# Stick-breaking attention as two lanes of 24 key blocks, and twelve projections as six pairs by seven products

## The chip, the core and the metric

The kernel runs on one core of a Trainium2 chip. Its engines are TensorE (PE, with its weight loads PEld), VectorE (DVE), ScalarE (ACT), GpSimd (POOL) and SyncE (SP), whose queue issues most of the DMAs. The metric is the device time of one execution in microseconds; lower is better. A time is given as the median of several runs.

## What is computed

One layer of a hybrid decoder trunk for 1024 tokens of width 1024, in float32. A normalised input goes through one input projection, and three mixers work on its parts: a state space model (SSD), stick-breaking attention and sparse attention (NSA). Each mixer's output is projected, scaled by a sigmoid gate, and summed; an output projection and a gated MLP follow. The edit touches the stick-breaking attention, the projections that feed it and the gates:

```python
def stick_breaking_attention(qkv):          # 4 heads of 128, blocks of 128 queries
    ...
    for i in range(s // SB_QBLK):
        q0 = i * SB_QBLK
        kl = q0 + SB_QBLK
        qb = q[:, :, q0:kl]
        zl = jnp.einsum('bhqd,bhkd->bhqk', qb, k[:, :, :kl]).astype(jnp.float32) * scale
        mask = jnp.arange(kl)[None, :] < (q0 + jnp.arange(SB_QBLK))[:, None]
        ls = jax.nn.log_sigmoid(zl)
        lk = jnp.where(mask, ls - zl, 0.0)
        later = lax.cumsum(lk, axis=3, reverse=True) - lk
        w = jnp.where(mask, jnp.exp(ls + later), 0.0)
        outs.append(jnp.einsum('bhqk,bhkd->bhqd', w.astype(v.dtype), v[:, :, :kl]))
...
        gm = jax.nn.sigmoid(merge_gate.astype(jnp.float32)).reshape(bsz, s, 3, D_MODEL)
        mixed = (gm[:, :, 0] * (y_ssm @ w_br_ssm[l]) + gm[:, :, 1] * (y_sb @ w_br_sb[l])
                 + gm[:, :, 2] * (y_nsa @ w_br_nsa[l])).astype(x.dtype)
```

## The kernel before

**Products.** Every float32 operand is split into a high and a low part, and a product is made of three matmuls (high by high, high by low, low by high). A *unit* is 128 output channels of the input projection: for each of two halves of 512 tokens, eight slices of 128 inputs times three matmuls, 48 matmuls of 128x512 into one bank `dense` (`fm_unit`; `half_unit` is the same as a generator that yields after every slice, three matmuls, so that other work can be put between: a *fine step*). `load_w` (lines 282 to 293) fetches a unit's weights on SP, copies the high part on ScalarE and subtracts on GpSimd (`whi`, `wlo`).

**Pairs.** `ssm_units` (line 586) does the 24 units of the SSD in twelve pairs: two units by two halves are a 2 by 2 block product, made with seven products of 12 matmuls each, 84 instead of 96. Its weights are combined in `weights7`, its inputs once in `combos` into the tiles `x`, 36 of them, which are given up at the end of this stage (`early.close()`).

**The stages.** The program goes through: input norm and the first projections; gate unit 0 and the SSD's twelve pairs; NSA, between whose matmuls the gate units 1 to 11 are filled in; the stick-breaking attention (`sb_stage`, line 1124); the SSD's scan; the branch projections, the output projection and the MLP. A gate tile is a `dense` bank through three ScalarE passes (`sigmoid`: exp, ln, exp, tile `gate_e`) and is stored to memory.

**The attention.** `project(h)` makes q, k and v of a head from three units, with the key columns 32 and 127 swapped, as six row tiles of 128x1024 (high and low part each; two sets of them exist). A `chain` is one head and one half c of the queries (512 columns) against key blocks of 128 from the last one down: eight blocks for c = 1, four for c = 0. A block goes through three steps: `score` (three matmuls into a bank, VectorE's minimum, ScalarE's exp and ln, its copy z, VectorE's maximum), `carry` (VectorE subtracts the row carried over from the block before, ScalarE and GpSimd split into `s_hi`, `s_lo`, two matmuls with a triangle sum up), `value` (VectorE adds the sum to z, ScalarE's exp, the split into `w_hi`, `w_lo`, three matmuls into the output bank). Blocks on the diagonal use 256 or 384 columns. A chain has two banks for scores (`ps_s` for c = 1, `ps_t` for c = 0) and one for its output (`ps_o`, `ps_b`). `attend(h)` takes one step of the chain c = 1 and, every second time, one of c = 0, and after each step some fine steps of a filler: the projection of the next head and two gates, at a rate of `SB_FILL` a step. Head 0's projection stands ahead of it without anything beside; behind each head what is left of its filler is finished before the next begins. Gates 12 to 23 are spread over the four heads, the last two behind a wait for value matmuls (`issue_after`).

A scheduler puts the recorded instructions in a static order per engine, and every engine works in that order. In NSA the order is as written.

Of the kernel before, what the change touches and what calls it, by code (L numbers as in the profile page):

```python
# [19 lines left out]
T = 1024  # L20
# [152 lines left out]
SB_GATES = (12, 14, 16, 18, 22, 24)  # L173

SB_LATE = 24
# [8 lines left out]
SB_FILL = (2.2, 2.2, 2.2, 2)  # L184
# [26 lines left out]
def trunk(ctx: ExitStack, tc: tile.TileContext, A: dict, outT: bass.AP, dbg=None):  # L211
# [362 lines left out]

    def gates(j0, j1, steps=unit_steps):
        for j in range(j0, j1):
            def evict(h, ps):
                e = gp.tile([128, 512], F32, name="gate_e")
                sigmoid(e, ps)
                nc.sync.dma_start(g_d[j * 128:(j + 1) * 128, hs(h)], e)  # L580
            yield from steps(U_GATE + j, evict)


    s_d = scratch("s_d", [24 * 128, T])

    def ssm_units():
# [26 lines left out]
        for q, m in itertools.product(range(4), (0, 2, 1)):  # L613
            u0 = 6 * q + 2 * m
            halos = [ev.tile([128, 4], F32, name="halo", bufs=4) for _ in range(2)]

            def evict(n, h, ps):
                o = ev.tile([128, 512], F32, name="o")
                if m < 2:
                    cu = q * 4 + 2 * m + n  # L620
                    conv(o, h, ps, [pvc(PV_CW, 4 * cu + 3 - d) for d in range(4)], pvc(PV_CB, cu), halos[n])
                act(o, o if m < 2 else ps, AF.Silu)
                nc.sync.dma_start(s_d[(u0 + n) * 128:(u0 + n + 1) * 128, hs(h)], o)

            w = weights7(wx, A["wfm"][U_SSM + u0], A["wfm"][U_SSM + u0 + 1], 512)
# [19 lines left out]

    ssm_units()
    tc.keep_in_program_order(nc.scalar.preload_act_table_set(TABLE))
# [476 lines left out]
def sb_stage(nc, tc, es, env):  # L1124
# [5 lines left out]

    def project(h, res):
        q_hi, q_lo, k_hi, k_lo, v_hi, v_lo = [row_t(n, R32) for n in range(6)]
        v_hi, v_lo = [x.rearrange("p (t d) -> p t d", d=128) for x in (v_hi, v_lo)]
        res.extend((q_hi, q_lo, k_hi, k_lo, v_hi, v_lo))

        def ev_q(c, ps):
            s = E.hs(c)
# [3 lines left out]
        def ev_k(c, ps):  # L1141
            s = E.hs(c)
# [7 lines left out]
        def ev_v(c, ps):  # L1150
            vT = hd.tile([128, 512], F32, name="half")
# [12 lines left out]
        for n, ev in enumerate((ev_q, ev_k, ev_v)):  # L1164
            yield from E.fine_steps(E.U_SB + 3 * h + n, ev)

    def chain(h, c, ps_z, ps_out, q_hi, q_lo, k_hi, k_lo, v_hi, v_lo):

        def tl(nm, dt=F32, bufs=None):
            return wk.tile([128, 512], dt, name=nm, tag=f"{nm}{c}", bufs=bufs)  # L1170

        po = ps_out()
        top = 4 * c + 3
        st = {}

        def cols(kb):
            j = kb - 4 * c
            return j, min(max(j, 0) * 128, 256), slice(kb * 128, (kb + 1) * 128)

        def strict(x, kb):  # L1180

            j, c0, _ = cols(kb)
# [4 lines left out]
        def score(kb):  # L1187
            _, c0, ks = cols(kb)
# [4 lines left out]
            mm(pz[:, c0:], k_lo[:, ks], q_hi[:, qs], start=False, stop=True)  # L1193
# [8 lines left out]
            strict(a, kb)  # L1202
            st[kb] = pz, a, z

        def carry(kb):
            _, c0, _ = cols(kb)
            pz, a, _ = st[kb]
            if kb < top:
                b0 = cols(kb + 1)[1]
                row = a[SWAP[0]:SWAP[0] + 1, b0:]  # L1210
                V.tensor_tensor(row, row, st[kb + 1][0][0:1, b0:], op=OP.subtract)
# [6 lines left out]
            mm(pz[:, c0:], E.neg_tri_r, s_lo[:, c0:], start=False, stop=True)  # L1218

        def value(kb):  # L1220
            _, c0, _ = cols(kb)
            pz, _, z = st[kb]
            V.tensor_tensor(z[:, c0:], z[:, c0:], pz[:, c0:], op=OP.add)
            act(z[:, c0:], z[:, c0:], AF.Exp)
            strict(z, kb)
# [4 lines left out]
            for n, (l, r) in enumerate(((v_hi, w_hi), (v_lo, w_hi), (v_hi, w_lo))):  # L1230
                last[0] = mm(po[:, c0:], l[:, kb, :], r[:, c0:], start=kb == top and n == 0, stop=kb == 0 and n == 2,
                   skip_group_check=True)
# [6 lines left out]
        y = wk.tile([128, 512], F32, name="ysb", bufs=2)  # L1239
        act(y, po, AF.Copy)  # L1240
        nc.sync.dma_start(E.y_d[(8 + h) * 128:(9 + h) * 128, c * 512:(c + 1) * 512], y)

    def attend(h, fill, late, *qkv):
        gens = [chain(h, 1, ps_s, ps_o, *qkv), chain(h, 0, ps_t, ps_b, *qkv)]
        n = m = i = 0
        while gens:
            for x in list(gens):
                if len(gens) == 2 and x is gens[1] and n % 2:
                    continue
                if next(x, 0) == 0:  # L1250
                    gens.remove(x)
                m += SB_FILL[h]
                fill.take(int(m))
                m -= int(m)
                i += 1
# [655 lines left out]
```

## Time and profile before

| | us |
|---|---|
| median of 3 runs | 2240.0 (2238.74 to 2242.33) |
| span of the profiled execution | 2244.0 |
| first to twelfth pair of the SSD, by product 3 | 108.4 to 317.2 |
| transposes of `nac` at the end of NSA | 814.1 |
| first score of the attention, `ps_t` and `ps_s` | 828.3 and 834.5 |
| last value product of the attention | 1148.3 |

The page gives the span, from the first to the last instruction, as the profiled execution's time; it stands 4.0 us above the median. PE, PEld, DVE, ACT and POOL are busy for 97, 77, 59, 54 and 57% of it. Matmuls are pipelined and overlap in the trace, and so do element passes that follow each other on one engine; the pace of an engine is then read from the distance of starts. The trace's windows give busy time with overlaps counted once, the granted TensorE clock (1.00 is full speed) and the share of the DMA engines. Rows of DMAs stand under SPq, the queue that issues them.

### The profile page before, as it was taken

Reading aid. Unit: us, or ns where it says so; the run is one execution under the profiler, and the core shown is the slowest. Engines: PE = TensorE matmul, PEld = TensorE weight load, DVE = VectorE, ACT = ScalarE, POOL = GpSimd, SP = SyncE. Lnnn points to the kernel's source line nnn. Section 1 sums busy time; section 2 is a strip of 40 time slices with the busy share of each in tenths; the row PEclk is TensorE's granted clock in tenths of the full one; section 3 lists DMA queues with packets and bytes.
Section 4 is the critical chain, followed back from the end, with each engine's and each line's share of the span. In section 5 each row is a group of like instructions: output and inputs, shape, how many; then the busy total and the mean of one; then the engine's idle time right before and its main releaser. Section 6 shows DMA issues by size and latency. Waiting matters only on the chain.

```text
span 2244.0 us, 30112 instructions
## 1 busy us (share of the span) xinstructions
PE 2167.6 (97%) x10589; PEld 1731.7 (77%) x10589; DVE 1314.7 (59%) x2419; ACT 1204.4 (54%) x2240; POOL 1269.3 (57%) x1122
## 2 busy tenths in 40 slices
PE   7999999999999999999999999999999999999997
PEld 7888889876666688888776678888778888878887
DVE  6765545257557426556537662228955767675776
ACT  6544442467757746667755531236644444575534
POOL 3777641146746734333337646568686777765743
PEclk9999999999999999999999999999999999999999
DMA  5233341321221011112262264235332323255433
GB/s 174 82 113 108 113 134 55 111 84 35 55 75 34 13 57 41 64 59 88 99 216 87 81 219 141 88 128 184 116 99 80 118 94 113 99 187 175 141 104 118
DMA packets 120104, 234.64 MB, mean 105 GB/s; under 512 B 28816, under 2 KB 43088, under 8 KB 119952
## 3 DMA queue, kind: packets, MB, share of 16 engines
q1 hardware_dynamic: 117072, 230.13, 31.2%
q10 hardware_dynamic: 2880, 2.59, 0.3%
q8 instruction: 83, 1.36, 0.3%
q14 instruction: 69, 0.57, 0.1%
HBM read 169.10 MB, written 63.57 MB: 104 GB/s over the span
## 4 chain that ended last, share of the span: by engine, by line
PE 80%; DVE 6%; ACT 4%; POOL 3%; issue 3%; DMA 2%; SPq 0%; DVEq 0%; ACTq 0%; POOLq 0%
PE dense L219 55%; PE ps_s L219 7%; PE ps_o L219 7%; PE ps_t L219 6%; PE ps_b L219 4%; PE psn L219 3%; DVE u L329 1%; POOL wlo L292 1%; POOL wlo L538 0%; DMA wraw<-in_wfm 0%; ACT dec L1302 0%; ACT wT L1000 0%; DMA traw<-in_wtm 0%; POOL h_lo L472 0%; DVE x L1530 0%
## 5 line engine op out<-in xcount | busy, mean ns | idle before, releaser
L292 POOL TENSOR_TENSOR wlo<-wraw,whi 128x256 fp32r<-128x256 f32 x344 | 273.1, 825 | 274.3 <-ACT whi L287 274.1
L219 PE MATMUL dense<-h_hi,whi 128*128 128x512 f32 x656 | 262.6, 400 | 0.0
L219 PE MATMUL dense<-h_hi,wlo 128*128 128x512 f32 x656 | 256.7, 392 | 1.2 <-POOL wlo L538 1.2
L219 PE MATMUL dense<-h_lo,whi 128*128 128x512 f32 x656 | 256.5, 391 | 0.0
L1011 POOL TENSOR_TENSOR wT_lo<-wT,wT_hi 128x512 fp32r<-128x512 f32 x132 | 168.8, 1288 | 84.8 <-ACT wT_hi L1010 76.5
L219 PE MATMUL dense<-hi,whi 128*128 128x512 f32 x576 | 214.5, 391 | 1.3 <-ACT whi L287 1.3
L219 PE MATMUL dense<-hi,wlo 128*128 128x512 f32 x512 | 200.8, 394 | 0.5 <-POOL wlo L292 0.4
L219 PE MATMUL dense<-x,uhi 128*128 128x512 f32 x600 | 191.8, 392 | 2.7 <-ACT uhi L546 1.5
L219 PE MATMUL dense<-lo,whi 128*128 128x512 f32 x448 | 176.1, 393 | 0.0
L287 ACT ACTIVATE whi<-wraw 128x1024 fp32r<-128x1024 f32 (+1 forms) x94 | 92.6, 985 | 154.4 <-PE dense L219 125.3
L547 POOL TENSOR_TENSOR ulo<-uf,uhi 128x1024 fp32r<-128x1024 f32 x38 | 91.8, 2416 | 115.0 <-ACT uhi L546 109.6
L219 PEld LDWEIGHTS dense<-h_hi,wlo 128*128 128x128 f32 x656 | 123.1, 188 | 27.9 <-POOL wlo L538 1.6
L219 PEld LDWEIGHTS dense<-h_hi,whi 128*128 128x128 f32 x656 | 123.7, 189 | 23.4
L219 PEld LDWEIGHTS dense<-h_lo,whi 128*128 128x128 f32 x656 | 123.5, 188 | 22.7
L219 PEld LDWEIGHTS dense<-x,uhi 128*128 128x128 f32 x600 | 112.4, 188 | 28.4 <-ACT x L610 2.4
L1215 POOL TENSOR_TENSOR s_lo<-sa,s_hi 128x512 fp32r<-128x512 f32 (+2 forms) x48 | 53.7, 1119 | 139.7 <-ACT s_hi L1214 139.7
L219 PEld LDWEIGHTS dense<-hi,whi 128*128 128x128 f32 x576 | 108.4, 188 | 25.5 <-ACT whi L287 2.1
L972 DVE TENSOR_REDUCE mx<-ps_t 128x1 f32<-128x384 f32 (+3 forms) x192 | 98.7, 520 | 48.9 <-PE ps_t L219 46.0
L329 DVE SCALAR_TENSOR_TENSOR u<-dense,pv,u 128x511 f32<-128x511 f32 (+1 forms) x140 | 103.5, 741 | 34.5 <-ACT u L325 34.5
L219 PEld LDWEIGHTS dense<-hi,wlo 128*128 128x128 f32 x512 | 96.3, 188 | 23.7 <-POOL wlo L292 2.0
L550 POOL TENSOR_TENSOR ulo<-uf,uhi 128x1024 fp32r<-128x1024 f32 x38 | 91.8, 2415 | 39.6 <-ACT uhi L549 38.0
L538 POOL TENSOR_TENSOR wlo<-wraw,whi 128x1024 fp32r<-128x1024 f32 x38 | 92.8, 2441 | 30.2 <-ACT whi L537 30.1
(555 smaller groups left out, 6088.4 us busy)
## 6 DMA issues: line engine op xcount, KB each, us to landing
wraw<-in_wfm SPq DMA_DIRECT2D x62, 512.0 KB, 3.7
wraw<-in_wup SPq DMA_DIRECT2D x52, 512.0 KB, 3.5
lo<-m_d SPq DMA_DIRECT2D x58, 256.0 KB, 3.2
g_d<-gate_e SPq DMA_DIRECT2D x48, 256.0 KB, 2.0
s_d<-o SPq DMA_DIRECT2D x48, 256.0 KB, 2.0
ge<-g_d SPq DMA_DIRECT2D x24, 512.0 KB, 3.4
m_d<-u SPq DMA_DIRECT2D x44, 256.0 KB, 2.0
row<-s_d SPq DMA_DIRECT2D x16, 512.0 KB, 5.0
```

Of the source, the lines that this page charges most:

```text
L219: i = f(*a, **k)
L287: act(hi, raw, AF.Copy)
L292: (V if tiles else P).tensor_tensor(lo[:, s], raw[:, s], fl(hi[:, s]), op=OP.subtract)
L329: V.scalar_tensor_tensor(o[:, d:], ps[:, :512 - d], taps[d], o[:, d:], op0=OP.mult, op1=OP.add)
L538: P.tensor_tensor(wlo, raws[0], fl(whi), op=OP.subtract)
L547: P.tensor_tensor(l24, f24, fl(h24), op=OP.subtract)
L550: P.tensor_tensor(l31, f31, fl(h31), op=OP.subtract)
L972: V.tensor_reduce(mx[:, h, a, n:n + 1], pm[:, :w], axis=AX, op=OP.max)
L1011: P.tensor_tensor(lo, wf, fl(hi), op=OP.subtract)
L1215: (P if SB_SLO else V).tensor_tensor(s_lo[:, c0:], a[:, c0:], fl(s_hi[:, c0:]), op=OP.subtract)
```

## The change

The units of gates 12 to 17 and of q, k, v of heads 0 and 1 are now made in six pairs behind the SSD's twelve, in the first stage. The gates' tiles go through `gate_out` as before. The heads' rows are stored to a scratch tensor `p_d`, and `fetch(h)` loads them in the attention stage, splits q and k, and transposes and splits v. Both fetches stand ahead of the chains.

The chains become two lanes of 24 blocks each, which go on from one head to the next: lane 0 does (head 0, c = 1), (1, 0), (2, 1), (3, 0); lane 1 does (0, 0), (1, 1), (2, 0), (3, 1). Both take all their steps in each of 26 turns. Left as filler are three gates, the units of heads 2 and 3, and three gates: twelve units, of which twelve fine steps stand ahead of the lanes. The rate of fill is 0.8 fine steps a step in turns 0 to 7, 2 in turns 8 to 15, and 0.7 behind; by turns 8, 12 and 16 at least 3, 6 and 9 units must be done. Every fill stands behind a matmul six marks back (`issue_after`).

```diff
-SB_GATES = (12, 14, 16, 18, 22, 24)
-
-SB_LATE = 24
+PAIR_GATES = 12, 18
+N_KEPT = 2
+SB_GATES = 18, 21, 24
+
+SB_DUE = {8: 3, 12: 6, 16: 9}
+SB_LEAD = 6
+SB_AHEAD = 12
...
-SB_FILL = (2.2, 2.2, 2.2, 2)
+SB_RATE = (0.8, 0.8, 2, 2, 0.7, 0.7)
...
+        tc.keep_in_program_order(nc.scalar.preload_act_table_set(TABLE))
+
+        def kept(u, h, ps):
+            o = ev.tile([128, 512], F32, name="o")
+            if u % 3 == 0:
+                act(o, ps, AF.Copy, scale=SB_SCALE)
+            else:
+                act(o, ps, AF.Copy)
+                dst, src = [x.rearrange("p (t k) -> p t k", k=128) for x in (o, ps)]
+                for m, n in (SWAP, SWAP[::-1]):
+                    act(dst[:, :, m], src[:, :, n], AF.Copy)
+            nc.sync.dma_start(p_d[u * 128:(u + 1) * 128, hs(h)], o)
+
+        for m, u in enumerate(range(0, 3 * N_KEPT, 2)):
+            pair(U_SB + u, m, lambda n, h, ps: kept(u + n, h, ps))
+        for m, j in enumerate(range(*PAIR_GATES, 2)):
+            pair(U_GATE + j, m, lambda n, h, ps: gate_out(j + n, h, ps))
...
+    def fetch(h, res):
+
+        rows = [row_t(n, R32) for n in range(6)]
+        for n in range(3):
+            r = (3 * h + n) * 128
+            nc.sync.dma_start(fl(rows[2 * n + 1]), E.p_d[r:r + 128, :])
+        for n in range(2):
+            hi, lo = rows[2 * n:2 * n + 2]
+            act(hi, fl(lo), AF.Copy)
+            V.tensor_tensor(lo, fl(lo), fl(hi), op=OP.subtract)
+            yield
+        hi, lo = rows[4:]
+        for c in range(2):
+            pt = E.psd.tile([128, 512], F32, name="dense", tag="dense")
+            for j in range(4):
+                s = slice((4 * c + j) * 128, (4 * c + j + 1) * 128)
+                tr(pt[:, j * 128:(j + 1) * 128], fl(lo[:, s]), ident)
+            act(hi[:, E.hs(c)], pt, AF.Copy)
+            V.tensor_tensor(lo[:, E.hs(c)], pt, fl(hi[:, E.hs(c)]), op=OP.subtract)
+            yield
...
-        for n in range(top + 3):
+        for n in range(len(blocks) + 2):
             for f, m in ((carry, n - 1), (value, n - 2), (score, n)):
-                if 0 <= m <= top:
-                    f(top - m)
-                    yield
...
+                if 0 <= m < len(blocks):
+                    f(m)
+                    yield True
+            yield False
...
+    marks = []
+    st = [[] for _ in range(4)]
+    for h in range(N_KEPT):
+        E.Fill(fetch(h, st[h])).rest()
+    fill = Units([gate(j) for j in range(SB_GATES[0], SB_GATES[1])] +
+                 [u for h in range(N_KEPT, 4) for u in project(h, st[h])] +
+                 [gate(j) for j in range(SB_GATES[1], SB_GATES[2])])
+    order = [[(0, 1), (1, 0), (2, 1), (3, 0)], [(0, 0), (1, 1), (2, 0), (3, 1)]]
+    lanes = [lane(l, [(h, c, kb) for h, c in hc for kb in range(4 * c + 3, -1, -1)], z, o)
+             for l, (hc, z, o) in enumerate(zip(order, (ps_s, ps_t), (ps_o, ps_b)))]
+    fill.ahead()
+    fill.take(SB_AHEAD)
+    due = 0
+    for t in range(26):
+        if t in SB_DUE:
+            fill.until(SB_DUE[t])
+        if t == 20:
+            E.ssm_rows(0, range(6))
+        on = list(lanes)
+        while on:
+            for x in list(on):
+                if not next(x):
+                    on.remove(x)
                     continue
...
+                due += SB_RATE[min(t // 4, 5)]
+                fill.ahead()
+                with tc.issue_after(marks[-SB_LEAD].ins) if len(marks) >= SB_LEAD else nullcontext():
+                    fill.take(int(due))
+                due -= int(due)
+    with tc.issue_after(marks[-1].ins):
+        fill.take(1000)
```

What this does to the order of instructions is shown at three places. The first is TensorE at the end of NSA, at the transpose of `nac` (the SSD's decay, the last matmul of that stage). Before:

```order
L219 MATMUL dense<-h_lo,whi 128x512
L219 MATMUL dense<-h_hi,wlo 128x512
L219 MATMUL dense<-h_hi,whi 128x512
L219 MATMUL ps_b<-ident,nac 128x128
L219 MATMUL dense<-h_lo,whi 128x512
L219 MATMUL dense<-h_hi,wlo 128x512
L219 MATMUL dense<-h_hi,whi 128x512
```

There `dense<-h_hi,whi` and its like are matmuls of head 0's projection. After the change:

```order
L223 MATMUL ps_b<-dta,tab 128x128
L223 MATMUL ps_b<-ident,nac 128x128
L223 MATMUL ps_s<-row_9348,row_9350 128x256
L223 MATMUL ps_s<-row_9349,row_9350 128x256
L223 MATMUL ps_t<-row_9348,row_9350 128x256
L223 MATMUL ps_t<-row_9349,row_9350 128x256
L223 MATMUL ps_s<-row_9348,row_9350 128x256
L223 MATMUL ps_s<-row_9349,row_9350 128x256
L223 MATMUL ps_t<-row_9348,row_9350 128x256
L223 MATMUL ps_t<-row_9349,row_9350 128x256
L223 MATMUL dense<-ident,row_9353 128x128 x8
L223 MATMUL ps_s<-row_9348,row_9351 128x256
```

Here `row_9348` and `row_9349` are the high and low part of head 0's q, `row_9350` and `row_9351` those of its k, `row_9353` and `row_9380` the fetched v of heads 0 and 1. The rows that follow the transpose of `nac` now all read fetched rows; the next dense matmul stands behind the sixteen transposes of v.

The second place is SP's queue there, after the change (`y_d<-yT` is NSA's last output, `ac_d` holds the decays):

```order
L1075 DMA y_d<-yT 128x2x128
L1145 DMA ac_d<-ac_9333 128x128
L1145 DMA ac_d<-ac_9334 128x128
L582 DMA g_d<-gate_e 128x512
L289 DMA wraw<-in_wfm 128x1024
L1162 DMA row_9349<-p_d 128x1024
L1162 DMA row_9351<-p_d 128x1024
L1162 DMA row_9353<-p_d 128x1024
L1162 DMA row_9376<-p_d 128x1024
L1162 DMA row_9378<-p_d 128x1024
L1162 DMA row_9380<-p_d 128x1024
```

Before, weight loads follow at this place; now the six fetches do, behind the store of the last filled gate half and the weight load of gate 20.

The third place is TensorE within the attention. Before, in head 2 with both chains under way (`row_9430` to `row_9433` are its q and k, `row_9434` and `row_9435` its v):

```order
L219 MATMUL ps_s<-row_9430,row_9432 128x512
L219 MATMUL ps_s<-row_9431,row_9432 128x512
L219 MATMUL ps_s<-row_9430,row_9433 128x512
L219 MATMUL ps_s<-s_hi,rtab 128x384
L219 MATMUL dense<-h_hi,whi 128x512
L219 MATMUL dense<-h_lo,whi 128x512
L219 MATMUL dense<-h_hi,wlo 128x512
L219 MATMUL dense<-h_hi,whi 128x512
L219 MATMUL ps_s<-s_lo,rtab 128x384
L219 MATMUL ps_o<-w_hi,row_9434 128x256
L219 MATMUL ps_o<-w_hi,row_9435 128x256
L219 MATMUL dense<-h_lo,whi 128x512
```

After, near the end, with lane 0 in head 3 (`row_10480` and `row_10481` its q, `row_10620` and `row_10621` its k, `row_10777` and `row_10778` its v):

```order
L223 MATMUL ps_s<-s_lo,rtab 128x256
L223 MATMUL ps_b<-w_lo,row_10777 128x512
L223 MATMUL ps_s<-row_10480,row_10620 128x384
L223 MATMUL ps_s<-row_10481,row_10620 128x384
L223 MATMUL ps_s<-row_10480,row_10621 128x384
L223 MATMUL ps_s<-s_hi,rtab 128x256
L223 MATMUL ps_s<-s_lo,rtab 128x256
L223 MATMUL dense<-h_hi,whi 128x512
L223 MATMUL dense<-h_lo,whi 128x512
L223 MATMUL dense<-h_hi,wlo 128x512
L223 MATMUL ps_o<-w_hi,row_10777 128x256
L223 MATMUL ps_o<-w_hi,row_10778 128x256
```

Before, dense matmuls stand between the two triangle matmuls and between the value products, and ten more follow the rows shown; after, three stand in the step. From the first score to the last value product the order has 1026 dense matmuls before and 546 after.

More of the change, by code (lines that the diff above doesn't have):

```diff
@@ L611, in snap, with pair @@
             return t
[L613 to L625, printed above, removed]
+        def pair(u, m, evict):
+            w = weights7(wx, A["wfm"][u], A["wfm"][u + 1], 512)
             x, y, z, v = ps_d(), ps_s(), ps_t(), (ps_o, ps_b)[m % 2]()
@@ L1185, in strict, with score @@
                 V.tensor_tensor(x[:, dg], x[:, dg], E.sb_mask[:, 256 - (dg.stop - c0):], op=OP.min)
-        def score(kb):
-            _, c0, ks = cols(kb)
+        def score(n):
+            h, c, _ = blocks[n]
+            _, c0, ks = cols(n)
+            q_hi, q_lo, k_hi, k_lo = st[h][:4]
             qs = slice(c * 512 + c0, (c + 1) * 512)
@@ L1239, in chain @@
[L1239 to L1248, printed above, removed]
-                    continue
[L1250 to L1255, printed above, removed]
-                if late and i > SB_LATE:
-                    with tc.issue_after(last[0].ins):
-                        late.take(2)
-            n += 1
@@ L1261, in sb_stage @@
[L1261 to L1275 removed]
+            for m, (x, y) in enumerate(((v_hi, w_hi), (v_lo, w_hi), (v_hi, w_lo))):
+                last = mm(po[0][:, c0:], x[:, kb, :], y[:, c0:], start=kb == top and m == 0, stop=kb == 0 and m == 2,
+                          skip_group_check=True)
@@ new lines, in value, with __init__, ahead, steps @@
+            marks.append(last)
+            if kb == 0:
+                y = wk.tile([128, 512], F32, name="ysb", bufs=2)
+                act(y, po[0], AF.Copy)
+                nc.sync.dma_start(E.y_d[(8 + h) * 128:(9 + h) * 128, c * 512:(c + 1) * 512], y)
+        for n in range(len(blocks) + 2):
+            for f, m in ((carry, n - 1), (value, n - 2), (score, n)):
+                if 0 <= m < len(blocks):
+                    f(m)
+                    yield True
+            yield False
+    class Units:
+        def __init__(self, units):
+            self.units, self.ready, self.cur, self.begun = list(units), [], None, 0
+        def ahead(self):
+            if self.units and not self.ready:
+                start, u, evict = self.units.pop(0)
+                self.ready.append((E.load_w(A["wfm"][u], 1024), start, evict))
+        def steps(self):
+            w, start, evict = self.ready.pop()
+            start()
+            self.begun += 1
+            for h in range(2):
+                out = []
+                yield from E.half_unit(E.psd, w, E.h_rhs, 8, h, out)
+                evict(h, out[0])
+        def step(self):
+            if self.cur is None:
+                self.ahead()
+                if not self.ready:
+                    return 0
+                self.cur = self.steps()
+            if next(self.cur, 0) != 0:
+                return 1
+            self.cur = None
+        def take(self, n):
+            while n > 0:
+                did = self.step()
+                if did == 0:
+                    return
+                n -= did or 0
+        def until(self, n):
+            while self.begun < n or self.cur:
+                self.step()
```

103 lines of the change are left out of this document (53 added, 50 removed).

## The prediction

> **What bounds the kernel now.** I read the page's totals first, then the chain of work that ended last, then windows over the two stages that the edit touches.
>
> ```profile
> span 2244.0 us, 30112 instructions
> ...
> PE 2167.6 (97%) x10589; PEld 1731.7 (77%) x10589; DVE 1314.7 (59%) x2419; ACT 1204.4 (54%) x2240; POOL 1269.3 (57%) x1122
> ...
> PE 80%; DVE 6%; ACT 4%; POOL 3%; issue 3%; DMA 2%; SPq 0%; DVEq 0%; ACTq 0%; POOLq 0%
> ```
> TensorE holds 80% of the chain, so a matmul less is worth its issue interval, as long as TensorE does not begin to wait. Matmuls overlap in the trace, so that interval is the distance of two starts:
>
> ```profile
> 803.15 0.39 PE L219 MATMUL dense<-h_hi,wlo 128*128 128x512 f32 x1
> 803.37 0.39 PE L219 MATMUL dense<-h_hi,whi 128*128 128x512 f32 x1
> 803.60 0.39 PE L219 MATMUL dense<-h_lo,whi 128*128 128x512 f32 x1
> ...
> 834.46 0.87 PE L219 MATMUL ps_s<-row,row 128*128 128x256 f32 x6
> ...
> 1148.29 0.39 PE L219 MATMUL ps_o<-w_lo,row 128*128 128x512 f32 x1
> ```
> A 128x512 matmul takes 0.2265 us of issue here. The last two rows are the first scores of the long lane and the last value product of the attention: its stage runs from 834.5 to 1148.5 us, 314.0 us. The windows show how full it is:
>
> ```profile
> core 0: us, PE busy (x) PEld busy (x) DVE busy (x) ACT busy (x) POOL busy (x), PEclk, DMA share, GB/s
> 127.74:317.18 189.44, 188.26 (x817) 152.85 (x816) 104.06 (x166) 88.82 (x130) 126.13 (x79) 1.00 0.33 109
> 828.28:1148.52 320.24, 315.08 (x1458) 259.08 (x1456) 180.73 (x331) 212.78 (x441) 116.92 (x134) 1.00 0.22 74
> 940.33:970.50 30.17, 28.88 (x138) 23.85 (x137) 25.68 (x47) 24.39 (x54) 13.29 (x14) 1.00 0.12 36
> ```
> The first is ten pairs of the seven-product stage (from the third product of one pair to that of the tenth after it): 18.94 us a pair, which is 84 matmuls at 0.2255 us, with ScalarE at 47% and GpSimd at 67%. The second is the attention: TensorE 98% busy, ScalarE only 66%, VectorE 56%. So before, the attention's element work is covered by dense projections and gates. The third is a stretch in which both chains of one head run: there VectorE is at 85% and ScalarE at 81%, and TensorE falls to 96%.
>
> **The change, part by part.**
>
> *Six pairs instead of twelve units.* Six pairs are added to the first stage: 6 x 18.94 = 113.6 us. Their extra ScalarE work (three passes for each of four gate tiles) has room beside 47%; the twelve stores of 256 KB and six loads of 512 KB have room beside a DMA share of 0.33; without that cover the passes would cost about 7 us a gate pair. Ahead of the first scores 120 of head 0's 144 dense matmuls go (the order has the last 24 behind them), and four transposes: -27.2 - 0.5 us. So the first score moves by 113.6 - 27.7 = +85.9 us, plus the wait that follows. Twelve plain units are 576 matmuls, six pairs 504: 72 x 0.2265 = 16.3 us less TensorE work in all.
>
> *The fetch.* Head 0 and 1 now come from memory, and TensorE's next row behind the transpose of nac reads them; before, dense rows stood there. The loads stand on SP behind the store of the last gate half and a weight load. The rows that price this:
>
> ```profile
> 807.43 1.06 ACT L287 ACTIVATE whi<-wraw 128x1024 fp32r<-128x1024 f32 x1
> 808.40 0.58 ACT L262 ACTIVATE gate_e<-dense 128x512 f32<-128x512 f32 x1
> ...
> 810.86 0.32 SPq L580 DMA_DIRECT2D g_d<-gate_e  x1
> 811.48 0.33 SPq L285 DMA_DIRECT2D wraw<-in_wfm  x1
> ...
> DMA to landing us min/median/max: 3.7/5.3/6.4
> ...
> L1428 DVE TENSOR_TENSOR row<-row,row 128x1024 fp32r<-128x1024 f32 x2 | 2.4, 1218 | 0.0
> ```
> Count from the last dense matmul of the gates. The weight copy ahead ends 1.0 us later, the gate's three passes and its store take 810.86 - 808.40 = 2.5 us more, the weight load follows, and the first row is issued at about 4.4 us. The landing line is that of four row loads of 512 KB in one burst (1057.5 to 1059.3 us); here the first two land after 4.9 and 5.7 us. Then ScalarE copies q and k (1.06 us each): first score at 11.7 us. TensorE has 2 us of its own until then, so it waits 9.7 us. The sixth row lands at about 15.4 us; its halves, VectorE's subtractions of 1.2 us and the two dense banks hold the next dense row to about 19.6 us, with 3.2 us of TensorE work since the first score: another 4.7 us. I take 14 us; the bounds are 8 (loads at the 3.7 us minimum, second wait hidden) and 17 (at 6.4 us). Queued behind TensorE's waiting row are all scores and all dense rows; nothing else can cover it.
>
> *The lanes.* 48 blocks stay 48, with the same passes. What goes is the half pace of the short chain and the ends between heads; what also goes is cover: between first score and last value 546 dense matmuls stand instead of 1026, twelve units fewer. I counted the order in 24 steps, from one score of lane 0 to the next, and gave each instruction its start-to-start time. Two such times, and the scores of a two-lane stretch:
>
> ```profile
> 966.12 0.65 ACT L1214 ACTIVATE s_hi<-sa 128x512 fp32r<-128x512 f32 x1
> 966.64 0.64 ACT L1224 ACTIVATE sz<-sz 128x512 f32<-128x512 f32 x1
> ...
> 950.30 0.69 DVE L1196 TENSOR_SCALAR sa<-ps_s 128x512 f32<-128x512 f32 x1 [0.52 <-PE ps_s L219]
> 950.90 0.64 DVE L1185 TENSOR_TENSOR sz<-sz,tab 128x128 f32<-128x128 f32 x1
> 951.67 0.69 DVE L1196 TENSOR_SCALAR sa<-ps_t 128x512 f32<-128x512 f32 x1
> ...
> 960.34 0.68 DVE L1196 TENSOR_SCALAR sa<-ps_s 128x512 f32<-128x512 f32 x1
> 960.94 0.41 DVE L1196 TENSOR_SCALAR sa<-ps_t 128x256 f32<-128x256 f32 x1
> ...
> 963.23 0.42 DVE L1196 TENSOR_SCALAR sa<-ps_t 128x256 f32<-128x256 f32 x1 [0.79 <-POOL wlo L292]
> ...
> 965.66 0.69 DVE L1223 TENSOR_TENSOR sz<-sz,ps_s 128x512 f32<-128x512 f32 x1
> ...
> 970.50 0.68 DVE L1196 TENSOR_SCALAR sa<-ps_s 128x512 f32<-128x512 f32 x1
> ```
> So 0.52 us for a ScalarE pass, 0.60 for one of VectorE. Sums over eight steps each, TensorE / ScalarE / VectorE: 60.5 / 53 / 50, then 82 / 52.5 / 53, then 56 / 55 / 55 us. Taking in each step the engine with most to do gives 64 + 82 + 61 = 207 us. The same count on the order of before gives 304 us against the measured 314.0, 3% short with TensorE first in most steps. In the new order TensorE leads clearly only in the middle third (heads 2 and 3 have to be projected there); in the outer thirds three engines are within a few us and each waits for the others, so 207 is a floor.
>
> The other price is the measured pace: from 950.30 to 970.50 us five scores start (three of 512 columns, two of 256; mean 410, and the 48 blocks' mean is 405): 4.04 us a block, 8.1 us a step of two lanes. The outer thirds at that pace, with step 1 at its 16.7 us of TensorE work and the end at the 15 us that a block needs from score to the update of z and the value product (950.30 to 965.66 for the first), give 73 + 82 + 72 = 227 us. I take 222, nearer the measured pace. The stage then falls by 314 - 222 = 92 us.
>
> *Sum.* +85.9 + 14 - 92 = **+8 us**. The tail is alike in both orders: 30 dense matmuls behind the last value product, then the scan. Against the profiled execution (the page gives its span, 2244.0 us; it is longer than all three timed runs, 2238.74 to 2242.33) that is 2252; against the median of 2240.0 it is **2248 us**.
>
> *The clock.* The long wait at the fetch may slow TensorE:
>
> ```profile
> 1155.00:1159.94 4.94, 2.66 (x12) 1.30 (x11) 1.34 (x3) 4.57 (x14) 2.44 (x3) 1.00 1.03 388
> 1159.94:1163.36 3.42, 3.42 (x18) 2.31 (x15) 0.98 (x3) 2.48 (x9) 1.46 (x2) 0.50 1.03 411
> ```
> After a window with TensorE idle for 2.3 of 4.9 us, the granted clock is 0.50 for 3.4 us. [...]
>
> **The rivals.**
>
> 1. *Faster: the matmuls saved arrive.* If backlogs even out over the lanes, the stage reaches its count of 207 us, and if the rows land at the burst's minimum the waits are 9 us: 85.9 + 9 - 107 = -12, **2228 us**. For it: ScalarE and VectorE sum to about 160 us each, far below 207. Against it: both were busy above 80% in the only two-lane stretch, and TensorE lost time there. It decides from a stage below 210 us.
> 2. *No difference.* The lanes run at the count plus the 3% of before, 214 us: 85.9 + 14 - 100 = 0, **2240 us**. For it: the count was that good before. Against it: before, TensorE led in nearly every step, so nothing else was tested.
> 3. *Slower by more: two score banks a lane.* A bank is held from the score to the update of z, 950.30 to 965.66 = 15.4 us, and about 1.5 us more for product and hand-over; with two banks a lane makes a block in 8.4 us at best. If every step that TensorE does not lead takes that or, with 256-column blocks queued behind full ones, a little more, the stage is 236 us: 85.9 + 14 - 78 = +22, **2262 us**. Against it: with fewer dense rows between them, a block's products come sooner.
>
> **How the numbers follow.** Forecast (2248; alone it would span 2245 to 2257): 0.45. Rival 1: 0.22. Rival 2: 0.20. Rival 3: 0.13. A measurement of this kernel tells about 0.2%, 4.5 us, from no change, so slower is 0.45 + 0.13 = 0.58, same 0.20, faster 0.22. The bounds of the two unknown terms (8 to 17, and 207 to 236) reach from -13 to +25 us; the range is 2229 to 2264.
>
> **What would show it.** The pairs: eighteen of them at 18.9 us, TensorE without gaps to the end of the eighteenth. The fetch: an idle TensorE of about 10 us ahead of the first score, released by ScalarE's copy of a row, and 4 to 5 us soon after. The lanes: 222 us from first score to last value product; TensorE at about 90% there, with waits for VectorE's update of z, its w_lo and GpSimd's s_lo in the outer thirds and hardly any in the middle. I am wrong if the first wait is under 5 us, if the outer thirds are as full of TensorE as the middle, or if the scan's start moves against the last value product.

## The result: slower by 1.1%, and the profile after

| | before | after |
|---|---|---|
| timed, median of 4 runs each (range) | 2239.42 us (2238.74 to 2242.33) | 2265.18 us (2261.56 to 2266.71) |
| ratio to before, 95% interval | | 1.0109 (1.0093 to 1.0124) |
| span of the profiled execution | 2244.0 us | 2262.2 us |
| last dense matmul of the gates ahead of the attention | 805.19 us | 924.64 us |
| first score of the long lane | 834.46 us | 937.04 us |
| last value product | 1148.29 us | 1167.93 us |
| scan's first matmul behind the plain units | 1157.57 us | 1177.26 us |

The forecast was 2248 us, slower, with a range of 2229 to 2264: the side was right, the size 17 us short and the time 1 us outside the range, at the end of what the bounds of its two unknown terms give (2240 + 25 = 2265). First the page of the changed kernel, its totals and its chain of work (busy time and share of the span of each engine; shares of the chain):

```profile
span 2262.2 us, 30108 instructions
...
PE 2162.0 (96%) x10517; PEld 1719.3 (76%) x10517; DVE 1333.0 (59%) x2431; ACT 1220.0 (54%) x2272; POOL 1315.1 (58%) x1122
...
PE 74%; DVE 8%; ACT 7%; issue 3%; POOL 3%; DMA 3%; SPq 0%; DVEq 0%; ACTq 0%; POOLq 0%
```
TensorE has 72 matmuls less, yet its share of the chain falls from 80% to 74%; VectorE, ScalarE and DMA take that place. The windows show where (start and end, length, busy time and count of each engine, granted clock, DMA share, GB/s): the fetch, the rest of it, and the thirds of the lanes.

```profile
927.11:937.04 9.93, 0.33 (x2) 0.14 (x2) 1.96 (x4) 3.27 (x5) 1.69 (x3) 0.54 0.80 288
937.04:945.06 8.02, 5.58 (x28) 5.23 (x28) 6.73 (x11) 6.11 (x15) 0.00 (x0) 0.71 0.37 151
945.06:1002.00 56.94, 54.13 (x238) 42.24 (x237) 43.20 (x83) 43.61 (x94) 20.21 (x22) 0.97 0.14 47
1002.00:1090.00 88.00, 87.69 (x415) 73.14 (x414) 60.64 (x116) 59.80 (x135) 35.95 (x40) 1.00 0.16 49
1090.00:1167.93 77.93, 68.14 (x299) 51.08 (x298) 66.10 (x115) 65.00 (x134) 29.28 (x28) 1.00 0.29 103
```
TensorE stands still for 9.6 us at the fetch, is full in the middle third and lacks 9.8 us in the last. The rows of TensorE around the fetch, and the copy of the row that it waits for (in brackets the idle time before an instruction and what ended it):

```profile
924.64 0.39 PE L223 MATMUL dense<-h_hi,wlo 128*128 128x512 f32 x1
...
927.11 0.33 PE L223 MATMUL ps_b<-ident,nac 128*128 128x128 f32 x1 [1.40 <-ACT dte L1138]
...
934.67 1.06 ACT L1165 ACTIVATE row<-row 128x1024 fp32r<-128x1024 f32 x1 [6.40 <-DMA row<-p_d]
...
937.04 0.80 PE L223 MATMUL ps_s<-row,row 128*128 128x256 f32 x2 [9.60 <-ACT row L1165]
...
944.56 0.70 PE L223 MATMUL dense<-ident,row 128*128 128x128 f32 x4 [2.44 <-DVE row L1175]
945.06 0.80 PE L223 MATMUL dense<-h_hi,whi 128*128 128x512 f32 x1
945.66 0.63 PE L223 MATMUL dense<-h_lo,whi 128*128 128x512 f32 x1
946.09 0.63 PE L223 MATMUL dense<-h_hi,wlo 128*128 128x512 f32 x1
```
The first score comes 12.4 us behind the last dense matmul of the gates, the next dense row 20.4 us behind it. The last two rows start 0.43 us apart and not 0.2265: the granted clock was 0.50 there, from 945.00 to 948.40 us.

In the last third TensorE waits in turn for all that the prediction named, and in the middle third for 0.3 us only (waits of TensorE's lines: us in total, times, longest):

```profile
PE ps_s L223 <- DVE sz L1280: 2.9, 4, 1.1
PE ps_s L223 <- POOL s_lo L1267: 2.2, 3, 1.3
PE ps_b L223 <- ACT w_hi L1285: 1.3, 2, 1.0
PE ps_t L223 <- DVE sz L1280: 1.2, 2, 0.8
PE ps_t L223 <- POOL s_lo L1267: 1.1, 2, 0.6
PE ps_o L223 <- DVE w_lo L1286: 0.7, 1, 0.7
```

### The profile page after: what moved, and what is told of

The parts are those of the page before. It is cut to its first block, busy times and chain, and to the rows that moved or that the text cites. A ratio compares the mean times of both kernels' runs of the same rounds, so it can differ in the third digit from the quotient of the medians.

```text
span 2262.2 us, 30108 instructions
## 1 busy us (share of the span) xinstructions
PE 2162.0 (96%) x10517; PEld 1719.3 (76%) x10517; DVE 1333.0 (59%) x2431; ACT 1220.0 (54%) x2272; POOL 1315.1 (58%) x1122
## 4 chain that ended last, share of the span: by engine, by line
PE 74%; DVE 8%; ACT 7%; issue 3%; POOL 3%; DMA 3%; SPq 0%; DVEq 0%; ACTq 0%; POOLq 0%
PE dense L223 48%; PE ps_o L223 7%; PE ps_s L223 7%; PE ps_t L223 6%; PE ps_b L223 4%; PE psn L223 2%; DVE u L333 1%; DVE sa L1253 1%; DVE sa L1263 0%; DVE sz L1280 0%; ACT sa L1249 0%; POOL wlo L542 0%; ACT h_hi L430 0%; ACT wT L1026 0%; ACT whi L291 0%
## 5 line engine op out<-in xcount | busy, mean ns | idle before, releaser
L296 POOL TENSOR_TENSOR wlo<-wraw,whi 128x256 fp32r<-128x256 f32 x296 | 238.6, 836 | 215.1 <-ACT whi L291 210.6
L223 PE MATMUL dense<-x,uhi 128*128 128x512 f32 x696 | 220.8, 390 | 2.9 <-ACT uhi L550 1.5
L223 PE MATMUL dense<-h_hi,whi 128*128 128x512 f32 x488 | 197.7, 405 | 0.8 <-DVE kk L794 0.8
L223 PE MATMUL dense<-h_hi,wlo 128*128 128x512 f32 x488 | 191.8, 393 | 1.1 <-POOL wlo L542 1.1
L223 PE MATMUL dense<-h_lo,whi 128*128 128x512 f32 x488 | 191.7, 393 | 0.0
L551 POOL TENSOR_TENSOR ulo<-uf,uhi 128x1024 fp32r<-128x1024 f32 x44 | 106.2, 2414 | 131.5 <-ACT uhi L550 123.5
L223 PEld LDWEIGHTS dense<-x,uhi 128*128 128x128 f32 x696 | 130.2, 188 | 32.2 <-ACT x L616 2.4
L554 POOL TENSOR_TENSOR ulo<-uf,uhi 128x1024 fp32r<-128x1024 f32 x44 | 106.2, 2413 | 43.4 <-ACT uhi L553 39.9
L223 PE MATMUL dense<-x,ulo 128*128 128x512 f32 x312 | 121.7, 391 | 0.3 <-POOL ulo L554 0.3
L1026 ACT ACTIVATE wT<-ps_s 128x512 f32<-128x512 f32 x132 | 78.3, 595 | 57.1 <-PE ps_s L223 53.0
L223 PEld LDWEIGHTS dense<-h_hi,wlo 128*128 128x128 f32 x488 | 92.0, 188 | 21.5 <-POOL wlo L542 1.6
```

The costliest lines, as they stand in the source:

```text
L223: i = f(*a, **k)
L296: (V if tiles else P).tensor_tensor(lo[:, s], raw[:, s], fl(hi[:, s]), op=OP.subtract)
L551: P.tensor_tensor(l24, f24, fl(h24), op=OP.subtract)
L554: P.tensor_tensor(l31, f31, fl(h31), op=OP.subtract)
L1026: act(w.rearrange("p h q -> p (h q)"), pz, AF.Exp)
```

## The experiments

The table gives what each profile shows: TensorE's idle time between the first score of either lane and the last value product, the scan's first matmul behind the plain units (two earlier steps of the scan stand among the last blocks in every kernel), and the length of what follows it. "Plain units" are the units of 48 dense matmuls that stand beside or behind the lanes; the rates of fill were set anew for them in each run. Nothing behind that matmul was edited in any kernel, so its start is the clean measure of an edit, and the column behind it shows what came by the way. A profile is one execution: the two of before differ by 1.9 us at the scan's start and by 5.4 behind it, so 2 or 3 us of the scan's start tell little. Ratios are to before, timed on the same chip.

| run | pairs added | plain units | idle in the stage | scan starts | behind it | timed median | ratio (95%) |
|---|---|---|---|---|---|---|---|
| before | 0 | 21 | 5.2 | 1157.6 | 1086.4 | 2239.42 | |
| before_again | 0 | 21 | 5.1 | 1155.7 | 1081.1 | 2238.51 (one run) | |
| the change | 6 | 12 | 15.4 | 1177.3 | 1084.9 | 2265.18 | 1.0109 (1.0093 to 1.0124) |
| lanes_alone | 0 | 21 | 3.5 | 1153.0 | 1087.2 | 2240.48 | 0.9998 (0.9988 to 1.0007) |
| pairs_alone | 6 | 12 | 38.2 | 1215.2 | 1087.0 | 2304.14 | 1.0279 (1.0263 to 1.0294) |
| heads_only | 3 | 18 | 4.3 | 1162.3 | 1083.3 | 2250.53 | 1.0036 (1.0024 to 1.0049) |
| gates16 | 5 | 14 | 9.1 | 1166.8 | 1075.9 | 2242.75 | 1.0000 (0.9984 to 1.0016) |
| all_kept | 6 | 12 | 13.0 | 1170.1 | 1096.9 | 2262.79 | 1.0086 (1.0068 to 1.0104) |
| snap_dve | 6 | 12 | 15.8 | 1176.5 | 1086.4 | 2265.69 | 1.0110 (1.0080 to 1.0139) |
| dense_ahead | 6 | 12 | 17.7 | 1175.7 | 1083.2 | 2260.90 | 1.0088 (1.0073 to 1.0103) |
| after_cover | 6 | 12 | 19.1 | 1171.8 | 1088.7 | 2264.93 | 1.0110 (1.0096 to 1.0124) |
| gates16_cover | 5 | 14 | 14.1 | 1163.7 | 1072.8 | 2235.76 | 0.9980 (0.9971 to 0.9989) |
| heads_cover | 3 | 18 | 8.0 | 1157.1 | 1086.6 | 2245.01 | 1.0018 (1.0009 to 1.0027) |
| split_late | 5 | 14 | 11.3 | 1164.2 | 1071.7 | 2233.42 | 0.9956 (0.9943 to 0.9970) |

**Half of the change at a time.** The lanes without pairs (head 0 projected ahead of them as before):

```diff
-PAIR_GATES = 12, 18
-N_KEPT = 2
...
+PAIR_GATES = 12, 12
+N_KEPT = 0
...
+    Units(project(0, st[0])).take(1000)
...
+    fill = Units(project(1, st[1]) + gs[0] + project(2, st[2]) + gs[1] + project(3, st[3]) + gs[2])
```


> The two endless lanes without any pair: head 0 projected ahead as before, heads 1 to 3 and twelve gates as plain fill, so as many matmuls as before. Theory (the loss comes from the fetch, the pairs' surplus and the cover that the pairs took away; the lanes by themselves cost nothing): TensorE stays full, 2234 to 2245 us, and the stage from first score to last value product is within 6 us of that before, counted with the dense rows behind it. Rival (two full lanes wait for each other whatever the cover): TensorE has waits of over 10 us in the stage, 2250 us or more.

And the pairs with the chains of before, `attend` head by head, heads 0 and 1 fetched:

```diff
-SB_GATES = (12, 14, 16, 18, 22, 24)
...
+SB_GATES = (18, 21, 21, 21, 23, 24)
...
-    E.Fill(project(0, st[0])).rest()
+    for h in range(N_KEPT):
+        E.Fill(fetch(h, st[h])).rest()
```


> The six added pairs and the fetch, but with the chains of before, head by head. Theory (the pairs take the cover away and the lanes win most of it back): the half-paced short chain and three more ends between heads leave TensorE without work, the stage is 255 to 275 us instead of 231, 2288 to 2310 us. Rival (the chains do as well as the lanes with so little cover): 2260 to 2270 us.

The lanes alone make no difference in time, and their scan starts 2.7 us earlier than in the second profile of before, hardly more than two profiles of one kernel differ; 3.5 us of idle TensorE are left in the whole stage. The pairs alone cost 2.8%. Two windows of that run (same columns as above), the whole stage and a late stretch of it:

```profile
939.63:1205.44 265.81, 227.64 (x973) 180.65 (x974) 177.04 (x323) 177.44 (x373) 83.28 (x90) 0.89 0.17 60
...
1165.80:1196.50 30.70, 17.20 (x39) 11.72 (x40) 17.60 (x28) 15.61 (x28) 6.10 (x5) 0.50 0.02 6
```
and the largest of TensorE's waits in the stage (us in total, times, longest):

```profile
PE ps_s L221 <- DVE sz L1269: 25.5, 11, 4.2
```
Where only one chain runs, each block waits up to 4.2 us for VectorE's update of z, and with no dense rows to fill these waits the granted clock was 0.50 for 30.7 us at a stretch. So neither half explains the loss by itself: the pairs and their fetch cost 59.5 us by the scan's start (1215.2 against 1155.7) where the chains of before have to run without cover, and the lanes win 37.9 of them back.

**How much cover.** Three pairs fewer (only those of the heads), then one fewer:

```diff
-PAIR_GATES = 12, 18
+PAIR_GATES = 12, 12
...
-SB_GATES = 18, 21, 24
+SB_GATES = 12, 18, 24
```


> The changed kernel without its three gate pairs: heads 0 and 1 in three pairs, twelve gates as plain fill, six in each outer third. Theory (cover decides): 36 matmuls less than before, 8 us, TensorE without gaps of over 5 us in sum in the lanes, only the fetch's 12 us of idle TensorE and its slower clock stay: 2241 - 8 + 14 = 2247 us. Rival (the lanes wait for each other whatever the cover once the rows come from memory): 2255 us or more.

```diff
-PAIR_GATES = 12, 18
+PAIR_GATES = 12, 16
...
-SB_GATES = 18, 21, 24
+SB_GATES = 16, 20, 24
```


> The changed kernel with one gate pair less: gates 16 and 17 are plain, one in each outer third of the lanes. A pair goes (19.1 us), 96 matmuls come (21.7 us). Theory (cover): the 10 us of idle TensorE in the last third and 3 us in the first are filled by them, 2265 - 19 + 22 - 10 = 2258 us. Rival (ScalarE's passes of two more gates hold the lanes as much as the matmuls fill): 2268 us or more.

Both behave as cover has it. With 18 plain units the lanes' idle time is 4.3 us, 2.5 of it at the fetch, and the whole is 3.5 us over the expected 2247. With 14 units it is 9.1 us, and the scan starts 10.5 us earlier than in the changed kernel, where a gain of 7 was expected. Ordered by pairs, the scan's start against before (1155.7): -2.7 us for none, +6.6 for three, +11.1 for five, +21.6 for six. The first five pairs cost 13.8 us together, the exposed fetch among it; the sixth, that of gates 16 and 17, costs 10.5 alone.

But the time of gates16 fell by 22 us, twice as much, and the other half lies far behind the attention. In the three kernels with five pairs TensorE's last 2650 rows, from 470 to 490 us behind the scan's start on, stand in one order, row for row the same in all three, which no other run has: 293 of the 2650 places differ from the changed kernel's, in the other runs 0 to 183. No line there was edited; the scheduler chose it. From the first of these rows to the end the three profiles take 595.7 to 596.6 us, the eleven others 608 to 611. In the changed kernel TensorE waits there (the three longest; same columns as above):

```profile
PE psn L223 <- DVE x L1798: 1.7, 1, 1.7
PE dense L223 <- ACT uhi L550: 1.5, 1, 1.5
PE psn L223 <- DVE u L333: 0.9, 1, 0.9
```
The window of the same stretch in the changed kernel:

```profile
1655.00:1720.00 65.00, 59.49 (x248) 46.88 (x248) 35.47 (x60) 30.86 (x45) 51.86 (x32) 0.97 0.25 82
```
and in gates16:

```profile
1640.00:1705.00 65.00, 65.00 (x289) 53.81 (x288) 43.85 (x76) 34.98 (x50) 55.60 (x38) 1.00 0.33 110
```
5.5 us of idle TensorE are gone there, and some 3 more near 2010 us: what is behind the scan takes 1071.7 to 1075.9 us in these three kernels, and 1081 to 1097 in all others. No run has that order and the attention of before.

**The same cover, spread.** All four heads' rows in the six pairs, the twelve gates as plain fill at an even rate, heads 2 and 3 fetched inside the lanes:

```diff
-PAIR_GATES = 12, 18
-N_KEPT = 2
...
+PAIR_GATES = 12, 12
+N_KEPT = 4
...
-SB_RATE = (0.8, 0.8, 2, 2, 0.7, 0.7)
+SB_RATE = (1.3, 1.15, 1.15, 1.15, 1.15, 1.0)
...
+    fill = Units([gate(j) for j in range(*SB_GATES)])
...
+        if t in SB_LOAD:
+            loads(*SB_LOAD[t])
+        if t in SB_SPLIT:
+            split[SB_SPLIT[t][0]].take(SB_SPLIT[t][1])
```


> The six pairs are the rows of all four heads (none of the gates); all twelve gates are plain fill, spread evenly over the lanes; heads 2 and 3 are fetched in steps 9 to 16 as their row buffers come free; 48 dense matmuls stand ahead of head 0's scores. As many matmuls as in the changed kernel. Theory (the loss is uncovered work: the fetch, and outer thirds of the lanes with too little dense work while the middle third has too much): TensorE has 192 us of work from first score to last value product and waits for 10 to 18 us, last value product at 1138 to 1146 us instead of 1168, in all 2235 to 2243 us. Rival (the lanes are bound by ScalarE and VectorE or by their two score banks, wherever the dense rows stand, or the two fetches inside wait for buffers): 2252 us or more.

My theory failed here by 20 us. The stage takes 221.2 us, 3.5 less than that of dense_ahead (below), and TensorE still idles 13.0 us in it, now in small waits throughout. So an even rate does not win the loss back. That too few matmuls are left for the whole stage fits this, but the run also has the work of two fetches more among the lanes, and TensorE was busy for 208.2 us there, where I had counted 192; how much each of these cost is open. Part of the rest is a slower start of the scan: its first 100 us in this run are

```profile
1170.10:1270.10 100.00, 91.78 (x500) 60.41 (x501) 58.60 (x130) 50.07 (x145) 55.87 (x53) 0.83 0.38 134
```
and in the changed kernel

```profile
1177.30:1277.30 100.00, 94.56 (x593) 64.26 (x593) 67.92 (x151) 55.74 (x159) 67.71 (x64) 0.95 0.34 122
```
500 matmuls against 593, at a granted clock of 0.83 against 0.95. Why the scan starts slower here was not tried; the profiled execution was the longest of the four timed (2268.69 us), so some of it may be this execution's alone.

**The pairs' surplus.** The copies of the added pairs on VectorE:

```diff
-            act(t, ps, AF.Copy)
+            if eng is V:
+                V.tensor_copy(t, ps)
+            else:
+                act(t, ps, AF.Copy)
```


> The changed kernel with the three copies per added pair on VectorE instead of ScalarE. Theory (the added pairs took 119.3 us instead of 113.6 because these copies queue behind the gates' three passes on ScalarE): the added pairs fall by about 4 us to 115 us, the whole to 2261 us. Rival (the surplus is the pace of the matmuls or the weights): pairs stay at 119 us, 2265 us.

The longest of the waits for such a copy in the changed kernel, from TensorE's rows:

```profile
377.48 0.39 PE L223 MATMUL ps_s<-h_hi,wlo 128*128 128x512 f32 x1
379.54 0.50 PE L223 MATMUL dense<-h_hi,uhi 128*128 128x512 f32 x1 [1.67 <-ACT x L616]
```
The same place in this run, and its last pair:

```profile
378.11 0.40 PE L223 MATMUL ps_s<-h_hi,wlo 128*128 128x512 f32 x1
378.59 0.50 PE L223 MATMUL dense<-h_hi,uhi 128*128 128x512 f32 x1
...
435.24 0.50 PE L223 MATMUL dense<-h_hi,uhi 128*128 128x512 f32 x1 [0.79 <-DVE x L617]
```
That wait goes, but another comes in the last pair for the copy on VectorE. From the third product of the twelfth pair to that of the eighteenth (322.67 to 436.42 us in the changed kernel, 323.29 to 435.24 here) it is 1.8 us less, half of what I expected, and the transpose of nac stands at 925.67 instead of 927.11 us. The time tells no difference: the runs span 2257 to 2275 us.

**The fetch.** First with dense rows recorded ahead of it:

```diff
-    for h in range(N_KEPT):
-        E.Fill(fetch(h, st[h])).rest()
     fill.ahead()
     fill.take(SB_AHEAD)
+    for h in range(N_KEPT):
+        E.Fill(fetch(h, st[h])).rest()
```


> The changed kernel with the first 36 dense matmuls of gate 18 recorded ahead of the fetch. Theory (the fetch is an exposed wait): TensorE idles 9.6 us ahead of the first score and 2.4 us at the v rows; 36 matmuls are 8.2 us, they fill most of the first wait, so about 8 us less than the changed kernel, 2257 us. Rival (these rows are needed as cover in the first steps of the lanes, and the wait only moves there): less than 3 us gained, 2262 to 2265 us.

The scan starts 1.6 us earlier, and the time is 4.3 us less, with ranges that overlap: by the scan's start a fifth of the 8 us, by the time about half. The dense rows went ahead of the transpose of nac, the store of ac and then the loads came later (first load issued at 935.2 us instead of 929.6), and 4.8 us of the first wait stayed. So the loads were brought back ahead and a whole gate put behind the transpose; this was tried on the change, on five pairs and on three:

```diff
-SB_AHEAD = 12
+SB_AHEAD = 16
...
+    kept = [loads(h) for h in range(N_KEPT)]
...
+    with tc.issue_after(E.nac_tr[0].ins):
+        fill.ahead()
+        fill.take(SB_AHEAD)
+    for h in range(N_KEPT):
+        E.Fill(fetch(kept[h], st[h])).rest()
```


> The changed kernel with all 48 dense matmuls of gate 18 (10.9 us) held behind the transpose of nac and ahead of the first score, and the six row loads issued as early as in the changed kernel. In the run with 36 dense rows ahead, these went before the transpose of nac, ac's store followed it 7 us later and the loads queued behind that store, so 4.9 us of the wait stayed. Theory (the exposed fetch costs its idle time and a slower clock): TensorE idle ahead of the first score under 2 us, no 13 us of half clock there; the scan starts at 1165 to 1169 us instead of 1177, 2253 to 2257 us in all. Rival (the rows are missed as cover in the lanes, whose first third then waits): the scan starts at 1173 us or later, 2261 us or more.

> One gate pair less (gates 16 and 17 plain), and the fetch covered in the same way. With one pair less the scan started at 1166.8 us, 10.5 us earlier than in the changed kernel; 10.8 and 2.7 us of idle TensorE at the fetch were left. Theory: both gains add up, the scan starts at 1155 to 1158 us, as in before (1156 and 1158), and the whole is 2233 to 2241 us, no more than before. Rival (cover taken from the lanes is missed there): 1163 us or later, 2244 us or more.

> Only the three pairs of heads 0 and 1, twelve plain gates, and the fetch covered in the same way. Without the cover the scan started at 1162 us, with 9.7 and 2.7 us of idle TensorE at the fetch and none to speak of in the lanes. Theory: these go, the scan starts at 1150 to 1153 us, 4 to 6 us before that of the kernel before, 2232 to 2238 us in all: the 36 matmuls saved (8.2 us) arrive once nothing is uncovered. Rival (the clock or ScalarE's split of the rows keeps TensorE waiting): 1158 us or later, 2244 us or more.

The first wait is gone in all three: after_cover has TensorE busy for the whole 11.04 us ahead of the first score. But the window behind it, until dense rows go on, is 9.3 us instead of 8.0:

```profile
926.00:937.04 11.04, 11.04 (x50) 9.14 (x51) 2.17 (x4) 4.91 (x9) 1.68 (x3) 1.00 0.76 275
937.04:946.34 9.30, 4.20 (x30) 3.35 (x28) 7.07 (x12) 9.30 (x22) 3.78 (x4) 0.83 0.62 226
```
TensorE's rows in that second window:

```profile
942.05 0.63 PE L223 MATMUL dense<-ident,row 128*128 128x128 f32 x4 [2.55 <-DVE row L1178]
943.73 1.11 PE L223 MATMUL dense<-ident,row 128*128 128x128 f32 x4 [1.06 <-DVE row L1178]
946.34 0.80 PE L223 MATMUL dense<-h_hi,whi 128*128 128x512 f32 x1 [1.49 <-DVE row L1178]
```
The transposes of v, four banks' worth for two heads, wait for VectorE, which splits these heads' rows in the same time, and the next dense row needs one of the banks. So part of the wait only moved: the scan starts 5.5, 3.1 and 5.2 us earlier with the cover (8 to 12 were expected), and of the three timed differences that of after_cover is nil (its part behind the scan is 3.8 us longer), those of the others 7 and 5.5 us. The time of gates16_cover came out as expected, but by luck: its scan starts where the rival had it, and the order behind the scan made up for that. With three pairs the kernel comes to 1.0018 of before, not below it as I expected.

Last, the split of v and of head 1 moved into steps 1 to 3, on top of gates16_cover:

```diff
+SB_SPLIT = {1: 0, 2: 1, 3: 1}
...
+    split = [E.Fill(fetch(kept[h], st[h])) for h in range(N_KEPT)]
+    split[0].take(2)
...
+        if t in SB_SPLIT:
+            split[SB_SPLIT[t]].take(2)
```


> One gate pair less and the covered fetch, and besides head 0's v rows are split and transposed in step 1 and head 1's rows in steps 2 and 3, between dense rows, instead of all ahead of the lanes. In the run with the covered fetch 6.4 us of idle TensorE were left just behind the first score, at the four banks of transposed v that wait for VectorE's subtraction. Theory: these fall below 2 us, the half clock of 6.8 us behind them goes too, the scan starts at 1156 to 1159 us instead of 1163.7, 2229 to 2233 us in all. Rival (VectorE and ScalarE are as full in the first steps, so that the lanes wait instead): 1162 us or later, 2234 to 2238 us. The rest behind the scan's start is expected to stay at 1073 us, as its order on TensorE is nearly that of the run with one gate pair less.

The rival's scan start came true, 1164.2 us: of the 5.6 us of idle TensorE in the 15 us behind the first score 1.9 are left, but the score itself comes 3.4 us later and the lanes wait in other places. The time of 2233.42 us is 0.44% below before and the best of all, yet its scan starts 8.5 us later than in before_again. It is faster only behind the scan's start, where its rows stand in the order of gates16.

**Which profile.** A second profile of the kernel before:

> The kernel before once more, for a second profile. The profiled execution of before had a span of 2244.0 us, 2245.7 us in the clock of the timed runs, against a median of 2241 us; the profiled difference of the two kernels was 18 us, the timed one 26 us. If that execution was a slow one, this one has a span of about 2239 us, and the clock or a stage shows where the other lost 5 us. If profiling itself costs this kernel 5 us, it is 2244 us again.

```profile
core 0: 2236.8 us, clock 0.994
```
This execution is 7.2 us shorter than the first one profiled: 1.8 ahead of the transpose of nac (812.25 against 814.08 us) and 5.4 behind the scan's start; the attention takes the same time in both. Against it the profiled difference is 25.4 us, as the timed one.

## Why the prediction was right in its side and short in its size

**Six pairs: mis-sized, by 6 us.** 113.6 us were forecast. The last matmul of the pairs moved by 119.3 us (439.10 against 319.77), the last dense matmul of the gates by 119.5 (924.64 against 805.19; behind it come the 120 rows of head 0). The two rows in the kernel before:

```profile
319.77 0.40 PE L219 MATMUL dense<-h_hi,ulo 128*128 128x512 f32 x1
...
805.19 0.39 PE L219 MATMUL dense<-h_hi,wlo 128*128 128x512 f32 x1
```
and in the changed kernel the last row of the pairs, and the window of the added pairs:

```profile
439.10 0.40 PE L223 MATMUL dense<-h_hi,ulo 128*128 128x512 f32 x1
...
320.76:440.73 119.97, 115.91 (x502) 93.50 (x500) 25.68 (x43) 57.73 (x105) 73.47 (x52) 1.00 0.32 108
```
More than half of the surplus was in the price. The window that I had taken for ten pairs, 840 matmuls, holds 817 (the trace has all 1008 rows of the twelve pairs): the order puts products of the next pair ahead of a pair's third product, and at the window's end, the twelfth pair, there was no next one. So a matmul took 189.44 / 817 = 0.232 us there and not 0.2255, and six pairs of 84 come to 116.9 us; in the added pairs it is 115.91 / 502 = 0.231. The rest is waits. All of TensorE's waits over 0.2 us in the added pairs, in one row:

```profile
PE dense L223 <- ACT x L616: 2.8, 3, 1.7
```
I had argued that ScalarE at 47% has room for the gates' three passes. It has, on average; but a copy that TensorE needs stands in ScalarE's order behind whatever comes first. Ahead of the longest wait, in a pair of the heads, ScalarE had itself waited for weights:

```profile
376.51 1.06 ACT L541 ACTIVATE whi<-wraw 128x1024 fp32r<-128x1024 f32 x1 [9.01 <-DMA wraw<-in_wfm]
377.47 0.58 ACT L662 ACTIVATE o<-ps_o 128x512 f32<-128x512 f32 x1
377.95 1.05 ACT L550 ACTIVATE uhi<-uf 128x1024 fp32r<-128x1024 f32 x1
378.89 1.07 ACT L616 ACTIVATE x<-dense 128x512 f32<-128x512 f32 x2
```
Only in the two shorter waits, 0.9 and 0.2 us, do passes of a gate stand ahead of the copy, as I had supposed in snap_dve for all. So the six pairs saved 11 us against the twelve plain units (576 x 0.2265 = 130.5), not the 16.3 of the forecast.

**The fetch: right.** Forecast: first score 11.7 us behind the last dense matmul, next dense row at 19.6. Measured: 12.4 and 20.4. The first wait was 9.6 us (forecast 9.7), released by ScalarE's copy of a row. The second was shorter, 2.44 instead of 4.7 us, because the scores and transposes ahead of it took longer, in part at half clock (0.50 from 937.04 to 941.60 us); VectorE set its end either way.

**The lanes: right within 5 us, and of the right kind.** 226.7 us were forecast from first score to last value product (222 and the 4.7 of the second wait); 230.9 were measured, with TensorE 93% busy, waits for z, w_lo, w_hi and s_lo in the outer thirds and 0.3 us in the middle. The first eight dense rows at half clock are 8 x 0.2 = 1.6 us of the miss, 2.5 are the lanes' own. The floor of 207 us (rival 1) was far off.

**The clock: taken as nothing.** The forecast's sum has no term for it. The window ahead of the score had a granted clock of 0.54, that behind it 0.71, and the half clock came back at 945.0 (0.50 from 945.00 to 948.40 us, 1.00 in the 3.4 us behind). Of this only the 1.6 us above are lost for certain, since VectorE held the rest up anyway.

**The base: a long execution.** In profiles the forecast was +8 and the result +18.2. The four steps are off by +5.9 (119.5 against 113.6, to the last dense matmul), +1.1 (from there to the first score: 29.3 us before, 12.4 after, so -16.9 against -18.0), +4.4 (the stage: 313.8 to 230.9 us is -82.9, against -87.3) and -1.4 (behind the last value product). Timed, the result is +25.8. The other 7 us are the difference of the two profiles of before. Against the second one the same steps are off by +7.7, +1.1, +4.4 and +3.9; what this adds, 1.8 and 5.3 us, lies in NSA and behind the attention, where no line was edited, and no run tells which of it is the change's.

**The rivals.** Rival 3 named 2262 us, close to the result, but its sum is not what happened: at two score banks a lane the stage was to be 236 us without the second wait, and it is 228 (230.9 - 2.4); the pairs' surplus made up for that by luck. Its mechanism is there in part. A row into `ps_s` or `ps_t` that waits for VectorE's update of z waits for its bank, and these are the largest of the waits in the last third, 4.1 of 9.4 us, and 25.5 us in pairs_alone. No run has another number of banks, so whether the banks or the work of ScalarE and VectorE hold the lanes there is open. Rivals 1 and 2 needed a stage of 207 and 214 us. What decides whether these waits show is the cover, as the experiments by halves and by pairs tell: the same lanes are nearly free of waits with 21 plain units, and the same pairs cost 59 us without the lanes.

## What to carry to other kernels

Work that is cheaper in an earlier stage (a pair here: 12 matmuls fewer, and some 2 us less as measured) is worth moving only as long as the stage that it leaves stays full without it; count what the other engines need there, and stop at the unit whose loss opens waits. Here none of the numbers tried (three, five and six) brought the scan's start ahead of that without any, 1153.0 us, and the sixth cost more than it saved. Where an edit shifts a scheduler's choices, compare starts of stages and the order behind them before crediting a time to the edit: the fastest kernel of this study wins by an order far behind the attention.

## What the hardware showed that I had not expected

TensorE's granted clock was halved right behind a window without one long idle stretch. In the changed kernel the two windows around 945 us are

```profile
941.60:945.00 3.40, 0.96 (x9) 0.70 (x7) 3.40 (x8) 3.40 (x12) 0.00 (x0) 1.00 0.00 0
945.00:948.40 3.40, 3.40 (x10) 2.66 (x9) 3.27 (x9) 2.26 (x7) 1.42 (x2) 0.50 0.03 7
```
TensorE was busy for 28% of the first, its longest pause 2.44 us, and the next 3.4 us went at half, 0.50 against 1.00. In pairs_alone it was busy for 56% of 30.7 us (17.20 of 30.70), with waits of 2.0 to 3.8 us, and the granted clock was 0.50 there. So a stretch of waits of 2 to 4 us ran at half clock from end to end. What brings the half clock on, and where a limit lies, no run here tells.
